# A 128-byte write by each DMA engine ahead of the first store of a streaming batch norm

## The chip, the cores and the metric

The kernel runs on one core of one Trainium2 chip. The metric is the device time of one execution in microseconds (us). It is limited by transfers: 537 MB go in and 537 MB go out.

## The reference

```
x: (32, 256, 128, 128) float32;  gamma, beta, running_mean, running_var: (256,)
out = gamma * (x - mean) / sqrt(var + 1e-5) + beta        # per channel
```

In the kernel this is one multiply and one add per element, with a scale and a shift per channel.

## The kernel before

The tensor is cut into 64 tiles of 128 channels x 16384 values (8 MB, 64 KB per partition). Three buffers go round. SyncE issues the loads, VectorE computes in place, ScalarE issues the stores. Each stream keeps one transfer in flight at a time; only the first two tiles' loads are queued without a wait.

```
nc.sync.dma_start(out=bufs[0][:, left], in_=xr[0][:, left]).then_inc(early, 16)   # a quarter of tile 0
zeroed = step(nc.vector.memset(rows[:], 0.0))
...                                        # four parameter loads of 16 rows x 1 KB
nc.sync.dma_start(out=bufs[0][:, right], in_=xr[0][:, right]).then_inc(loaded[0], 16)
for i in range(1, NT):
    s, turn = i % NBUF, i // NBUF
    if turn:
        nc.sync.wait_ge(stored[s], 16 * turn)              # the buffer is free
    inst = nc.sync.dma_start(out=bufs[s][:], in_=xr[i]).then_inc(loaded[s], 16)
    if i >= 2:
        inst._wait_ge(loaded[(i - 1) % NBUF], ...)         # the load before has landed
...                                        # scale and shift are made on VectorE and ScalarE
compute(0, left)._wait_ge(early, 16)
compute(0, right)._wait_ge(loaded[0], 16)
store(0, 2)                                                # a DMA issued by ScalarE
for i in range(1, last):
    compute(i)._wait_ge(loaded[i % NBUF], ...)
    turn_of_store(i)                                       # the store before has landed
    store(i, i + 2)
...                                        # the last tile is shared by VectorE and ScalarE
```

## Time and profile before

| | before |
|---|---|
| time, median of the first 3 runs | 2483.66 us (2483.18 to 2484.57) |
| span of the profiled execution | 2484.7 us |
| VectorE busy | 564.0 us (23%) |
| DMA queue of the loads / of the stores | 50.1% / 49.9% of the 16 engines' span |

The lines of the page that show this stand in the prediction. Two more things are used later. The first is what SyncE's DMA issues waited for, in the view of the DMA queue's own waits (us in total, times, longest). Line 98 waits for the load before, line 97 for the store that frees the buffer:

```profile
SPq L98 <- DMA t<-in_x_dram: 1378.8, 62, 48.0
SPq L97 <- DMA out_dram<-t: 1009.0, 61, 16.8
```

Each load waits for both, one after the other: first some 16.5 us for the store (1009.0 / 61), then some 22 us more for the load before (1378.8 / 62). So it is the load before that releases a load; its buffer has then been free for 22 us.

The second is the record of each DMA packet in the trace (start, duration, size, queue). A 64 KB packet is one row of a tile, and takes 2418 ns undisturbed. The records name no engine, but on a saturated engine each packet starts where the one before ended, so joining ends to starts gives sixteen rows. This is one of them around the first store (L load packet, S store packet; start in us + duration in ns):

```
before   L29.77+2419  L32.20+3072  S35.27+2418  L37.68+2418  S40.09+2418 ...
```

The load packet right before the first store packet is 654 ns too long. All 16 engines have such a packet, too long by 0.60 us on average. I call this "the stall before store 0" from here on; its size is always the excess over the undisturbed duration, summed over 16 engines' packets and divided by 16. Durations taken as undisturbed are 2418, 1815 and 608 ns for packets of 64, 48 and 16 KB.

### The profile page before, as it was taken

To read this page: it belongs to the slowest core of one execution; us is meant where nothing else is said; L and a number is where in the kernel's file an instruction comes from. 1 tells how busy PE (TensorE), PEld (TensorE's weight loads), DVE (VectorE), ACT (ScalarE), POOL (GpSimd) and SP (SyncE) were. 2 spreads that over 40 slices of the span, in tenths; PEclk is the share of its full clock that TensorE was granted. 3 is DMA by queue.
4 is the path that set the end of the run, shared out by engine and by line. 5 is a ranking of instruction groups with operands and counts; after the bars stand their busy time and mean duration, and the time that the engine had idled before them with its cause. 6 is when DMAs were issued, how large, how long until landed. Compare 5 with 4: busy or idle time off the path is not lost.

```text
span 2484.7 us, 389 instructions
## 1 busy us (share of the span) xinstructions
DVE 564.0 (23%) x76; ACT 7.9 (0%) x3; POOL 0.2 (0%) x4
## 2 busy tenths in 40 slices
DVE  3121221212212222122221221212212122121221
ACT  0000000000000000000000000000000000000001
POOL 0000000000000000000000000000000000000000
DMA  9999999999999999999999999999999999999999
GB/s 422 423 439 434 430 436 435 437 428 437 435 436 432 433 438 429 436 434 431 434 427 437 437 426 439 436 432 430 436 438 430 433 427 438 430 430 437 436 426 406
DMA packets 18707, 1073.84 MB, mean 432 GB/s; under 512 B 2128, under 2 KB 2192, under 8 KB 2192
## 3 DMA queue, kind: packets, MB, share of 16 engines
q1 hardware_dynamic: 9488, 536.94, 50.1%
q10 hardware_dynamic: 9216, 536.88, 49.9%
q14 instruction: 3, 0.02, 0.0%
HBM read 536.94 MB, written 536.87 MB: 432 GB/s over the span
## 4 chain that ended last, share of the span: by engine, by line
DMA 99%; ACT 0%; SPq 0%; issue 0%; DVE 0%; DVEq 0%
DMA t<-in_x_dram 99%; ACT t L154 0%; SPq L87 0%; DVE rows L85 0%; SPq L91 0%; DVE eps_t L103 0%; DVEq L190 0%; SPq L66 0%
## 5 line engine op out<-in xcount | busy, mean ns | idle before, releaser
L126 DVE TENSOR_SCALAR t<-t,scale_t,shift_t 128x16384 f32<-128x16384 f32 (+2 forms) x65 | 560.5, 8624 | 1886.5 <-DMA t<-in_x_dram 1886.4
L154 ACT ACTIVATE t<-t,shift_t,scale_t 128x7168 f32<-128x7168 f32 x1 | 6.4, 6361 | 2442.7 <-DMA t<-in_x_dram 2442.7
L104 DVE STREAM_TRANSPOSE turned<-rows 32x1024 f32<-32x1024 f32 x1 | 1.2, 1233 | 7.1 <-DMA rows<-in_running_mean_dram 7.1
L111 ACT ACT_TABLE_LOAD x1 | 1.3, 1283 | 0.9 <-SPq L66 0.9
L85 DVE MEMSET rows<- 32x1024 f32 x1 | 0.9, 912 | 1.2 <-SPq L66 1.2
L109 DVE COPY par<-turned 32x8 f32<-32x8 f32 x4 | 0.6, 162 | 0.1
L111 ACT ACTIVATE std_t<-par,eps_t 128x2 f32<-128x2 f32 x1 | 0.3, 295 | 9.2 <-DVE par L109 9.2
L118 DVE RECIPROCAL rstd_t<-std_t 128x2 f32<-128x2 f32 x1 | 0.2, 166 | 0.4 <-ACT std_t L111 0.4
L121 DVE TENSOR_TENSOR shift_t<-par,ms_t 128x2 f32<-128x2 f32 x1 | 0.2, 163 | 0.0
L120 DVE TENSOR_TENSOR ms_t<-par,scale_t 128x2 f32<-128x2 f32 x1 | 0.2, 161 | 0.0
L119 DVE TENSOR_TENSOR scale_t<-par,rstd_t 128x2 f32<-128x2 f32 x1 | 0.2, 161 | 0.0
L179 POOL MEMSET const-bfloat16-1.0<- 128x1 bf16 x1 | 0.1, 102 | 0.0
L179 POOL MEMSET const-uint8-127<- 128x1 uint8 x1 | 0.1, 101 | 0.0
L179 POOL MEMSET const-float32-0.0<- 128x1 f32 x1 | 0.1, 99 | 0.2 <-issue 0.2
L179 POOL MEMSET const-float32-1.0<- 128x1 f32 x1 | 0.1, 98 | 0.0
L103 DVE MEMSET eps_t<- 128x1 f32 x1 | 0.1, 59 | 0.1
## 6 DMA issues: line engine op xcount, KB each, us to landing
t<-in_x_dram SPq DMA_DIRECT2D x1, 6144.0 KB, 19.4
t<-in_x_dram SPq DMA_DIRECT2D x1, 2048.0 KB, 7.6
out_dram<-t ACTq DMA_DIRECT2D x64, 38.6
t<-in_x_dram SPq DMA_DIRECT2D x63, 38.6
rows<-in_running_var_dram SPq DMA_DIRECT2D x1, 16.0 KB, 6.4
rows<-in_gamma_dram SPq DMA_DIRECT2D x1, 16.0 KB, 6.2
rows<-in_beta_dram SPq DMA_DIRECT2D x1, 16.0 KB, 5.9
rows<-in_running_mean_dram SPq DMA_DIRECT2D x1, 16.0 KB, 5.9
```

What stands on the lines that cost most here:

```text
L85: zeroed = step(nc.vector.memset(rows[:], 0.0))
L103: step(nc.vector.memset(eps_t[:], eps))
L104: step(nc.vector.transpose(out=turned[:], in_=rows[:]), fetched, 16 * NPAR)
L109: placed = step(nc.vector.tensor_copy(out=flat[q * B : (q + 1) * B], in_=blocks[:, :, q, 0]))
L111: nc.scalar.activation(out=std_t[:], in_=var_t, func=mybir.ActivationFunctionType.Sqrt, bias=eps_t[:], scale=1.0,)._wait_ge(vec, placed).t ...
L118: step(nc.vector.reciprocal(out=rstd_t[:], in_=std_t[:]), act, 1)
L119: step(nc.vector.tensor_mul(out=scale_t[:], in0=gamma_t, in1=rstd_t[:]))
L120: step(nc.vector.tensor_mul(out=ms_t[:], in0=mean_t, in1=scale_t[:]))
L121: ready = step(nc.vector.tensor_sub(out=shift_t[:], in0=beta_t, in1=ms_t[:]))
L126: return nc.vector.tensor_scalar(out=t[:, cols], in0=t[:, cols], scalar1=scale_t[:, cb : cb + 1], scalar2=shift_t[:, cb : cb + 1], op0=myb ...
L154: nc.scalar.activation(out=t[:, VCOLS:], in_=t[:, VCOLS:], func=mybir.ActivationFunctionType.Identity, bias=shift_t[:, cb : cb + 1], scale ...
L179: nc = _bacc.Bacc("TRN2", target_bir_lowering=False, num_devices=1)
```

## The change

It means to take this first-store stall out of the stream of loads: each engine writes 128 bytes of zeros early, and store 0 covers them later. (Such a small early write is called a touch below.) Store 0 waits until they have landed, so that the order of the two writes is safe.

```
+    blank = params.tile([NE, B], f32, name="blank", tag="blank")          # 16 x 32
+    touched = tc.alloc_semaphore("touched")
...
+        blanked = step(nc.vector.memset(blank[:], 0.0))
+        nc.scalar.dma_start(out=outr[0][0 :: P // NE, 0:B], in_=blank[:])._wait_ge(vec, blanked).then_inc(touched, 16)
...
         compute(0, right)._wait_ge(loaded[0], 16)
+        nc.scalar.wait_ge(touched, 16)
         store(0, 2)
```

## The prediction

> **What bounds the kernel now.** I read the page first (busy shares, slices, queues, chain), then the windows view, the timeline of the first microseconds, the chain of waits in order of time, and last the DMA packet records of the trace one by one.
>
> ```profile
> span 2484.7 us, 389 instructions
> ## 1 busy us (share of the span) xinstructions
> DVE 564.0 (23%) x76; ACT 7.9 (0%) x3; POOL 0.2 (0%) x4
> ...
> DMA  9999999999999999999999999999999999999999
> ...
> q1 hardware_dynamic: 9488, 536.94, 50.1%
> q10 hardware_dynamic: 9216, 536.88, 49.9%
> ...
> DMA 99%; ACT 0%; SPq 0%; issue 0%; DVE 0%; DVEq 0%
> ```
>
> VectorE works 23% of the time. The 16 DMA engines are busy in every one of the 40 slices, and the two queues (q1 carries the loads that SyncE issues, q10 the stores that ScalarE issues) add up to 100% of the engines' time. So a microsecond is saved only if each DMA engine spends a microsecond less on its packets, or starts earlier, or ends closer to the end of the span.
>
> ```profile
> 0.00:2.00 2.00, 0.79 (x1) 1.10 (x1) 0.20 (x4) 1.00 0.07 16
> 2.00:4.00 2.00, 0.18 (x2) 0.18 (x1) 0.00 (x0) 1.00 0.98 344
> ...
> 80.00:2450.00 2370.00, 537.56 (x61) 0.00 (x0) 0.00 (x0) 1.00 1.00 433
> ...
> 2482.00:2484.70 2.70, 0.00 (x0) 0.00 (x0) 0.00 (x0) 1.00 0.00 0
> ```
>
> The last two columns are the DMA share and GB/s. The engines are idle for about the first 2.0 us and about the last 1.6 us, and saturated from 2 us on, before the first store exists. From the packet records: 16,256 packets of 64 KB take 2.418 us when nothing disturbs them. All of the data in such packets is 1073.74 MB / (16 x 64 KiB) = 1024 packets per engine, x 2.418 = 2476.0 us. Startup 2.0 and the tail 1.6 make 2479.6. The remaining 5.1 us of the span of 2484.7 are packets that took longer than 2.418 us, plus the small packets: summed over the records and divided by 16, the excess of load packets is 5.2 us (64 KB), 0.28 (48 KB) and 0.49 (16 KB), that of store packets 0.11. That is 6.1, 1 us more than the 5.1, since the records overlap slightly (on average 16.03 are open for 16 engines). This slack of some 5 to 6 us, 0.24% of the time, is all that any change to how packets flow can touch.
>
> **What the change aims at.** Listed by start, the excess has a peak just where the first store begins. Store 0 is issued at 30.04 us:
>
> ```profile
> 23.33 6.68 DVE L126 TENSOR_SCALAR t<-t,scale_t,shift_t 128x12288 f32<-128x12288 f32 x1 [8.31 <-DMA t<-in_x_dram]
> 30.04 78.75 ACTq L137 DMA_DIRECT2D out_dram<-t  x3
> 52.87 8.81 DVE L126 TENSOR_SCALAR t<-t,scale_t,shift_t 128x16384 f32<-128x16384 f32 x1 [22.86 <-DMA t<-in_x_dram]
> ```
>
> Its first 16 packets (one per engine) start 5.0 us after the issue; those of the next two stores start 4.0 us after theirs. The 16 load packets that stand right before them, one per engine, are long by 227 to 844 ns, 9.77 us in sum, so 0.61 us per engine. At the second, third and fourth store nothing of the kind stands in the records (excess per 20 us slice under 0.03 us). So something about the first write costs every engine about 0.61 us once. The change moves that first write ahead, to a 128-byte one.
>
> **What the Trainium skill says.** The page "DMA: Bandwidth & Descriptors", section "Queues, rings and completion order": each engine serves its queue rows in turn and switches only at packet boundaries. The trace agrees: packets of q1 and q10 fill the engines without overlap. The section "Why a DMA increments its semaphore by 16 and not by 1" says that the outermost size decides how many engines share a transfer: 16 rows make 16. The parameter loads of 16 rows agree: 64 packets of 1 KB for four of them, 16 each. Its section "Specifications" says that the engine does a read-modify-write for transfers under 512 B; this trace has no data write of that size. No page tells of a cost of an engine's first write; that stall is known here from the records alone.
>
> **The change part by part.**
> 1. One more memset on VectorE (16 x 32). The eps memset beside it takes 0.06 us; as every step waits for the one before, the setup chain becomes longer by about 0.1 us. That chain ends at 12.6 us, but the parameter transposition before it waits until 9.36 us for the fourth parameter load, so it is hidden there.
> 2. One more DMA issue on ScalarE. It takes about 0.35 us (the store issues take 0.34 to 0.37) and waits for the memset, so it starts at about 2.3 us. The built program shows it ahead of the activation table load, which goes from 0.90 to about 2.7 us and ends at 4.0; its result is wanted at 11.41. Hidden.
> 3. A wait for the landing of the 128-byte rows ahead of store 0. They land by about 6 to 10 us (parameter loads of 16 KB took 5.9 to 6.4 us to land); the store is ready at 30.04. Costs nothing.
> 4. Sixteen more data packets and 16 semaphore packets, one of each per engine. A 1 KB packet takes 46 ns and a semaphore packet 9 ns, so at most 0.06 us per engine.
> 5. The first-write stall at 35.5 us goes: -0.61 us.
> 6. The first-write stall comes back at the new place. The first load's issue starts at 0.95 and its first packet at 2.0 us, so the blank packet comes at about 2.3 + 1.0 = 3.3 to 3.5 us, when the engines have had load packets for 1.4 us (DMA share 0.98 in the window 2 to 4 us). There each engine does its own cold start: the first 16 load packets are long by 0.42 us on average, and end at 2.8 to 3.5 us. If the write stall falls into that, part is hidden; if it comes after, 0.61 is paid again, only earlier. Behind the small parameter packets the first 48 KB packets are long by 0.12 to 0.36 us, so a small transfer in the stream can cost such a bubble too: up to +0.28 us.
> Sum: -0.61 + 0.06 + (0 to 0.61) + (0 to 0.28), so -0.55 to +0.34 us. The middle is -0.1; I lean to some overlap and take -0.2.
>
> **The rivals.** (a) The stall is only moved: the engines are the bound at both places and never idle between, so the time stays at 2483.7 +- 0.3. For it: the share of 0.98 in the window in which the blank write arrives. (b) The stall is hidden in the startup of the reads or shrinks with a small packet: -0.55 us, 2483.1. For it: the cold reads of that very moment, and that a 128-byte packet holds little behind it. (c) The cost belongs to a store beside a 64 KB load packet, or to the first page of the output rather than the engine's first write, and appears at the first true store nevertheless: +0.06 to +0.3, 2483.9. Against it: stores 1 to 3 show none. (d) A new wait delays store 0 by a slow read-modify-write: it would need over 20 us to be felt, against 6 us for loads of 16 KB. Very unlikely. In none does the time move by even 0.05%.
>
> **Range and chances.** I predict 2483.66 - 0.2 = 2483.4 us. The spread of the runs is larger than the effect: the three runs cover 1.4 us, the profiled execution took 2486.4, and most of the 5.2 us of long load packets stand in irregular places (for example 1140 to 1300 us and 2040 to 2210 us), which may differ by run. So the range is 2482.2 to 2485.4. A change of 2% would be 49.7 us, nine times all of the slack there is, and a loss of that size would need the engines idle for 50 us, for which nothing is added. Faster 0.01, same 0.98, slower 0.01.
>
> **What would show it.** In the changed kernel's packet records: 16 packets of 128 B on q10 at about 3.5 us; the load packets around 35 us back to 2.418 us and store 0 first seen 4.0 to 4.4 us after its issue, not 5.0 (step 5 right); load packets around 3 to 6 us long by more than before (step 6, rival a) or not (rival b). If the packets before store 0 are still long, rival c holds. DMA share, queues and the chain stay at 99 to 100%. A change of over 2 us in the median of fast runs would prove the reading wrong.

## More of the kernel before

In the steady state a store is issued 16.9 us after a load and the next load 21.7 us after that (medians of the issue times). The two streams are staggered by about half of the 38.7 us that a tile takes.

## The result

| | before | changed |
|---|---|---|
| median of 6 runs | 2484.03 us | 2483.23 us |
| lowest to highest | 2482.88 to 2485.29 | 2482.53 to 2489.46 |
| span of the profiled execution | 2484.7 us | 2480.7 us |

The ratio of the fast runs is 1.0001, with a 95% interval of 0.9988 to 1.0014: the same. A ratio is the mean time of one kernel's fast runs over that of the other's of the same rounds, so it is not quite the ratio of the medians above; here one run of 2489.46 lifts the mean of the changed kernel.

The page of the changed kernel, in the parts that the prediction showed of the one before:

```profile
span 2480.7 us, 392 instructions
## 1 busy us (share of the span) xinstructions
DVE 564.1 (23%) x77; ACT 7.9 (0%) x3; POOL 0.2 (0%) x4
...
DMA  9999999999999999999999999999999999999999
...
q1 hardware_dynamic: 9488, 536.94, 50.0%
q10 hardware_dynamic: 9248, 536.88, 49.9%
...
DMA 99%; ACT 0%; issue 0%; SPq 0%; DVE 0%; DVEq 0%
```

One more VectorE instruction and 32 more packets on the store queue; nothing else has moved. The windows view (start and end, length, then engines, and at the end DMA share and GB/s):

```profile
0.00:2.00 2.00, 0.79 (x1) 0.00 (x0) 0.20 (x4) 1.00 0.18 41
2.00:4.00 2.00, 0.27 (x3) 1.28 (x1) 0.00 (x0) 1.00 0.97 328
...
80.00:2450.00 2370.00, 537.57 (x61) 0.00 (x0) 0.00 (x0) 1.00 1.00 434
...
2478.00:2480.70 2.70, 0.00 (x0) 0.00 (x0) 0.00 (x0) 1.00 0.00 0
```

The idle ends are as they were, and the middle runs at 434 GB/s against 433. The timeline of the changed kernel, at the start and around store 0 (start, length, engine, instruction):

```profile
2.18 0.09 DVE L105 MEMSET blank<- 16x32 f32 x1
2.30 0.38 ACTq L106 DMA_DIRECT2D out_dram<-blank  x1
...
2.71 1.28 ACT L117 ACT_TABLE_LOAD   x1 [2.71 <-DVE eps_t L109]
...
23.41 6.68 DVE L132 TENSOR_SCALAR t<-t,scale_t,shift_t 128x12288 f32<-128x12288 f32 x1 [8.25 <-DMA t<-in_x_dram]
30.12 0.36 ACTq L143 DMA_DIRECT2D out_dram<-t  x1
```

The write is issued at 2.30 us and the activation table is loaded after it, without harm. The page's part on DMA issues has the landing, 5.8 us after the issue, 22 us before anything asks for it:

```profile
out_dram<-blank ACTq DMA_DIRECT2D x1, 2.0 KB, 5.8
```

Now the packets around store 0, on one engine of each kernel:

```
before   L29.77+2419  L32.20+3072  S35.27+2418  L37.68+2418
changed  L29.80+2421  L32.22+3118  S35.33+2418  L37.74+2418
```

The stall is still there, at the same place. Over all 16 engines it was 0.60 us before and 0.75 us in the changed kernel. The early write itself left no mark: its 16 packets started between 5.74 and 6.99 us and took 13 ns each, and the 16 KB load packets of 5 to 8 us were long by 0.02 us in sum (0.04 before). The first 48 KB packets, at 7.6 to 8.1 us, were long by 0.28 us per engine (0.25 before).

Why then is the span 4.0 us shorter? The excess of all 64 KB load packets was 5.21 us per engine in the trace of before and 1.26 in the one of the changed kernel, 3.95 less. Before, most of it stood in places such as 1140 to 1300 us (1.2 us) and 2000 to 2240 us (1.4 us). The second trace of the kernel before (e8_before_again) and two variants of the changed kernel, below, tell whether the change has to do with this.

### The profile page after: what moved, and what is told of

It is laid out like the page before. It is cut to its first block, busy times and chain, and to the rows that moved or that the text cites. A ratio compares the mean times of both kernels' runs of the same rounds, so it can differ in the third digit from the quotient of the medians.

```text
span 2480.7 us, 392 instructions
## 1 busy us (share of the span) xinstructions
DVE 564.1 (23%) x77; ACT 7.9 (0%) x3; POOL 0.2 (0%) x4
## 4 chain that ended last, share of the span: by engine, by line
DMA 99%; ACT 0%; issue 0%; SPq 0%; DVE 0%; DVEq 0%
DMA t<-in_x_dram 99%; ACT t L161 0%; SPq L89 0%; DVE rows L87 0%; SPq L93 0%; DVE blank L105 0%; DVE eps_t L109 0%; DVEq L197 0%; SPq L68 0%
```

## The experiments

The question is why the early write did not take the stall away, and what the stall is. Two theories stood at first: the touch reached the wrong rows or came at the wrong time (then all rows, or a later touch, would help), or it was too small (then only a large early write would help). A third was that the stall isn't tied to the store at all. e1 to e3 and e9 to e12 are edits of the changed kernel; e4 to e7 are edits of the kernel before, without the 128-byte write, and e8 is the kernel before itself. In e4, e6 and e7 the load of tile 2 also waits for the early transfer, since that one uses its buffer.

### e1_shift: store 0 comes 10 us later

```
         nc.scalar.wait_ge(touched, 16)
+        for k in range(8):        # eight activations of 128x1024 on a tile that nobody uses
+            ...
         store(0, 2)
```

> The changed kernel with eight idle activations (128x1024, about 1 us each) on ScalarE ahead of store 0, so that store 0 is issued some 8 to 9 us later, at about 39 us, still within load 1. In the changed kernel the 16 load packets right before store 0 were long by 0.74 us per engine although the 128-byte rows had been written. If this stall belongs to the arrival of the first large store, the 16 long packets move with it to about 43 to 45 us and again cost 0.4 to 0.9 us per engine. If it belongs to a place in the run or in load 1, long packets stay at 33 to 36 us and those before store 0 are 2.418 us.

Store 0 was issued at 39.81 us. No load packet at 33 to 36 us was long, so the stall belongs to the store, not to a place in the run. But the store came just as the load of tile 1 ended. Its own first packets were long instead, by 0.69 us per engine. This can't be told from what later stores met in this run: each but the last has long packets, of 0.5 to 1.0 us per engine in sum. The run took 2587.87 us, 4.2% more than the kernel before on the same chip (2484.41). A delay of 10 us in one store cost 103 us. The timeline shows the new order (SPq issues loads, ACTq stores; x2 stands for two issues, from the start of the first to the end of the second):

```profile
39.81 41.46 ACTq L145 DMA_DIRECT2D out_dram<-t  x2
42.94 40.64 SPq L101 DMA_DIRECT2D t<-in_x_dram  x2
```

A store and the next load are now issued 3 us apart (2.4 us in the median later), no longer half a tile apart, and it stays so. The waits of SyncE's DMA issues (line 100 for the store, line 101 for the load before):

```profile
SPq L100 <- DMA out_dram<-t: 2288.8, 61, 38.5
SPq L101 <- DMA t<-in_x_dram: 188.4, 62, 38.1
```

A load now waits some 37.5 us for the store and then only 2.5 us for the load before (without the first wait of 38.1). It is still the load before that releases it, and each store is released by the store before; as a tile takes 40.4 us in both streams, the offset between them stays as it is. Both streams end and start anew within 2.4 us of each other, tile after tile, and most of the long packets stand at these starts: the excess in this trace is 48.3 us per engine on loads and 51.8 on stores, together 100.0 against 6.1 before, which is 93.9 of the 103 us. The windows view has 416 GB/s from 100 to 2500 us, in place of 433.

### e2_all_rows: 128 bytes to every row

```
-    blank = params.tile([NE, B], ...)          +    blank = params.tile([P, B], ...)
-    out=outr[0][0 :: P // NE, 0:B]             +    out=outr[0][:, 0:B]
```

> The changed kernel with the early write going to all 128 rows (128 bytes each, 8 packets per engine) with the same split over engines as the store, in place of every eighth row. If the 16-row touch failed because its rows fall to other engines than those that the store gives them to, the packets before store 0 go back to 2.418 us (stall under 0.1 us per engine). If a small write does not open what the first large store pays, the stall stays at 0.5 to 0.9 us per engine.

The stall before store 0 was 0.65 us, on all 16 engines. Which rows were touched was not what was wrong.

### e3_late_touch: the 128 bytes at 23 us

```
+        nc.scalar.wait_ge(loaded[0], 16)
         nc.scalar.dma_start(out=outr[0][0 :: P // NE, 0:B], in_=blank[:])...   # moved here, ahead of store 0
```

> The changed kernel with the 128-byte write issued only when load 0 has landed (about 23.4 us) in place of 2.3 us, so that it comes to the engines within 64 KB load packets and only some 8 us before store 0. If the early touch worked but was forgotten in the 29 us until store 0, the stall before store 0 goes (under 0.1 us), and may show up before the touch at about 27 us. If it is the first write that arrives behind 64 KB load packets that stalls them, whatever its size, the stall moves to about 27 us (0.5 us or more). If only a large write pays, it stays before store 0 at 0.5 to 0.9 us and nothing is long at 27 us.

The 16 small packets started at 27.4 to 27.8 us, 8 us before store 0, among load packets of 64 KB. None of those was long, and the stall before store 0 was 0.65 us. The touch was not forgotten; it had paid for nothing.

### e4_full_row: one 64 KB row per engine

```
+        nc.gpsimd.memset(bufs[2][0:NE, :], 0.0).then_inc(zeros, 1)      # the third buffer, not yet loaded
+        nc.scalar.dma_start(out=outr[0][0 :: P // NE, :], in_=bufs[2][0:NE, :])._wait_ge(zeros, 1).then_inc(touched, 16)
```

> The changed kernel with the early write being one whole 64 KB row per engine (16 rows of zeros from the still unused third buffer, zeroed by GpSimd), issued at about 18 to 22 us, during load 0. If the stall is a one-time cost of an engine's first large write, 16 load packets become long before it (0.4 to 0.9 us per engine at about 20 to 26 us) and those before store 0 are 2.418 us. If each first use of particular rows or of the first tile's buffer pays, the stall before store 0 stays at 0.5 to 0.9 us. The extra 1 MB adds 2.4 us to the time in either case.

Load packets before the early write were long by 0.55 us at 16 to 18 us, so a large write does meet the stall early. But store 0, which came at 41.7 us, met one of 0.49 us again. This fits neither expectation, and the run isn't clean: the 16 rows all came from partitions 0 to 15 and took up to 7.2 us in place of 2.4, an excess of 3.3 us per engine, and the load packets of 26 to 29 us, as they ended, were long by another 0.38. At this point "a long stretch of loads alone brings the stall back" was a theory of its own.

### e5_split_store: a part of store 0 comes early

```
-        store(0, 2)
+        nc.scalar.dma_start(out=outr[0][:, left], in_=bufs[0][:, left])._wait_ge(done, 1).then_inc(touched, 16)
+        nc.scalar.dma_start(out=outr[0][:, right], in_=bufs[0][:, right])._wait_ge(done, 2).then_inc(stored[0], 16)
```

> The kernel before with store 0 cut in two: its first quarter (128 rows of 16 KB) is issued when computed, at about 15 us, the rest at about 30 us. Theory G (the stall comes when a queue gets a large transfer after the engines have served only the other queue for a long time): load packets are long before the first part, at about 17 to 20 us (0.3 to 0.8 us per engine), and the second part, which comes some 5 us after the end of the first, finds no stall (under 0.15 us). Theory W (every first write to other bytes of the output by an engine pays): both parts pay 0.4 us or more. The time stays within 0.1% of before in either case.

(It has no blank write, and the fourth load also waits for the first part.) The first part met the stall in two portions, 0.17 us at 17 us and 0.45 us at 22 us, together 0.62; the second part met none. So it is one sum of about 0.6 us, paid once, and with packets of 16 KB it isn't paid all at the first of them. This speaks against a payment at every first write to other rows.

### e6_load_on_act and e7_quarter_touch: a load and a store at the same moment

```
e6  +   nc.scalar.dma_start(out=bufs[2][:, left], in_=xr[2][:, left]).then_inc(touched, 16)
e7  +   nc.scalar.dma_start(out=outr[0][:, left], in_=bufs[2][:, left])._wait_ge(zeros, 1).then_inc(touched, 16)
```

> The changed kernel with the early write replaced by an early load on ScalarE's queue: a quarter of tile 2 (128 rows of 16 KB), issued at about 12 us. If the stall comes from a second queue that starts while the other one is being served, whatever the direction, the load packets around 13 to 17 us are long by 0.3 us or more per engine. If it comes from writing to HBM, nothing is long there (under 0.1 us) and the stall before store 0 at about 32 to 38 us is as before (0.5 to 0.8 us). The extra 2 MB cost 4.8 us in the time.

> As e6_load_on_act, with a store of the same size at the same moment on the same queue (zeros from the unused third buffer to the first quarter of each row of tile 0). If writing is what stalls, the load packets at about 13 to 17 us are long by 0.3 to 0.8 us per engine here and not in e6_load_on_act. Then store 0 comes some 10 to 15 us after the end of this store: if one large write were enough for the whole run, the packets before it are 2.418 us; if a long stretch of loads alone brings the stall back, they are long by 0.3 to 0.8 us per engine. The extra 2 MB cost 4.8 us.

Both were issued on ScalarE's queue, with 2 MB, right after the same activation:

```profile
11.33 0.38 ACTq L150 DMA_DIRECT2D t<-in_x_dram  x1
```

```profile
11.55 0.37 ACTq L152 DMA_DIRECT2D out_dram<-t  x1
```

(The first line is of e6_load_on_act, the second of e7_quarter_touch, both from the timeline.) With the load, the load packets of 11 to 24 us were long by 0.03 us in sum, and the stall before store 0 was 0.68. With the store they were long by 0.66 us, and store 0 met none (0.00). A second queue that begins to work did not stall the first here; a write did. And this write paid for the later ones.

### e8_before_again: the kernel before once more

> The kernel before once more, unchanged, for a second trace. The stall before store 0 should be 0.5 to 0.8 us per engine again. The sum of all long load packets was 6.0 us per engine in the first trace of it and 2.2 in the one of the changed kernel; if that is a matter of the run and not of the change, it will differ here from 6.0 by a microsecond or more, or equal it by chance, and the time will move with it.

The stall before store 0 was 0.64 us. The excess of all load packets was 6.22 us against 5.98 in its first trace, at partly other places: 0.6 us at 740 to 760 us, where the first trace had none, and 0.2 in all at 1140 to 1300 us, where the first had 1.2. Of the changed kernel's variants, e2_all_rows had 6.36 and e3_late_touch 6.71. The low 2.22 of the changed kernel's own trace is therefore not what a 128-byte touch does; the 4.0 us between the two spans are the difference of two executions. The untraced times say so too: the fastest run of the kernel before (2482.88 us) is 0.35 us above the traced run of the changed one (2482.53), and in the rounds of e9 to e12 the kernel before once took 2489.65.

### e10_rows_4k and e11_rows_1k: how much must be written

```
-    blank = params.tile([NE, B], ...)     +  blank = params.tile([P, 1024], ...)    # e11: [P, 256]
-    out=outr[0][0 :: P // NE, 0:B]        +  out=outr[0][:, 0:1024]                 # e11: 0:256
```

> The changed kernel with an early write of 4 KB to each of the 128 rows, split over the engines as the store is (8 packets, 32 KB per engine), issued at about 3 us. So far: 128-byte touches paid nothing and saved nothing, a quarter of a tile (16 KB to each of 128 rows) paid 0.65 us once and freed store 0, which came 7 us after its end; a full row per engine (16 rows) paid 0.55 and store 0, 17 us later, paid 0.49 again. Theory D (dose: the stall is paid over the first 20 to 40 KB that an engine writes, once): about 0.5 us per engine of long load packets at 6 to 22 us, and under 0.15 before store 0. Theory F (a stretch of some 15 us of loads alone brings it back): the same at 6 to 22 us, and again 0.5 to 0.8 before store 0. Theory L (only packets of 16 KB and more pay): nothing extra early and 0.5 to 0.8 before store 0.

> As e10_rows_4k with 1 KB to each row (8 KB per engine), issued at about 2.5 us. Theory D: a part of the stall early (0.1 to 0.3 us per engine) and the rest before store 0 (0.3 to 0.5). Theories F and L: 0.5 to 0.8 before store 0 whatever was paid early.

One engine of e10_rows_4k, early and around store 0 (its 4 KB store packets, of 159 ns, are left out):

```
e10   L4.46+611  L5.10+935  L6.04+1032  L7.36+813 ...  L31.61+2419  L34.02+2429  S36.45+2418  L38.86+2418
```

With 32 KB per engine in packets of 4 KB, the 16 KB load packets of 5 to 9 us were long by 0.94 us per engine (0.02 to 0.05 in the kernels with early touches of 128 bytes), and store 0, some 30 us later, met none. So the stall is moved by this touch. Not all of the 0.94 comes on top: the first 48 KB load packets, long by 0.2 to 0.4 us per engine without such a write, are long by 0.02 here. Over all load packets of the first 14 us the excess is 1.60 us, and 1.41 in e12_far_rows, against 0.75 to 1.06 in the kernels with no early write or one of 128 bytes. The difference, some 0.4 to 0.8 us, is about what store 0 is spared (0.60 to 0.75). The touch also takes 8 x 159 ns = 1.27 us of each engine. The load of the rest of tile 0, on which the compute waits, lands 2.1 us later, and so store 0 is issued at 32.25 us in place of 30.12:

```profile
25.54 6.68 DVE L132 TENSOR_SCALAR t<-t,scale_t,shift_t 128x12288 f32<-128x12288 f32 x1 [8.96 <-DMA t<-in_x_dram]
32.25 0.34 ACTq L143 DMA_DIRECT2D out_dram<-t  x1
```

With 8 KB per engine in packets of 1 KB (e11_rows_1k), 0.14 us was paid at 5 to 9 us on 16 KB packets, nothing over all load packets of the first 14 us (0.79), and store 0 met 1.18 us, more than without any touch. Theory D expected a remainder of 0.3 to 0.5 us, so it is wrong in this: the payment isn't shared out in proportion to bytes. Whether the amount per engine counts (over 8, at most 32 KB) or the size of a packet (over 1, at most 4 KB), these two runs do not tell, because both sizes grew together. Neither can be the whole of it: one packet of 64 KB per engine (e4_full_row) is above both and did not free store 0.

### e9_rows_4k_later: a longer stretch of loads alone

```
-            if i >= 2:                    +            if i > 2:          # the load of tile 2 no longer waits for tile 1
+        eight short activations ahead of store 0, as in e1_shift
```

> As e10_rows_4k, with store 0 held back by eight short activations (8 to 9 us) and the load of tile 2 issued without waiting for tile 1, so that loads follow one another without a gap and the stretch of loads alone between the early write and store 0 is 9 us longer than in e10_rows_4k. Theory D: no stall before store 0 (under 0.15 us) if e10_rows_4k has none. Theory F: 0.5 to 0.8 us before store 0, which then stands at about 43 to 46 us. Theory L as in e10_rows_4k. The time itself may be longer by up to 4%, as in e1_shift, where the same delay put loads and stores in step.

1.07 us was paid at 5 to 9 us on 16 KB packets, and the load packets right before store 0, at 46.2 us, were not long (0.01). Some 38 us of loads nearly alone did not bring the stall back, so that theory falls. What store 0 met in e4_full_row remains unexplained. My bound for the time was wrong: the run took 3030.45 us, 22% more, not 4%. The second load of the two queued at the start lands early. From then on a load is released by the landing of a store, which also releases the next store, and the streams fell into step still more tightly (x3: from the start of the first to the end of the third):

```profile
93.67 102.28 ACTq L143 DMA_DIRECT2D out_dram<-t  x3
93.68 102.22 SPq L100 DMA_DIRECT2D t<-in_x_dram  x3
```

Store and load were issued 0.01 us apart, and a tile took some 51.5 us. From about 1800 us on the load before landed just after the store, the next load was issued 0.1 us after the next store, and a tile took 42.7 us. Why so small an offset should matter stays open. The page shows both halves:

```profile
DMA  9898989888898989898889889999999999999999
GB/s 389 312 350 315 342 309 338 313 330 328 317 340 319 340 312 345 304 339 318 336 309 339 312 346 388 388 409 389 391 385 393 403 386 388 393 407 390 385 386 407
```

The span is 544 us longer than in the trace of the kernel before. The packets' records add up to 2763.7 us per engine, 280 more than there, nearly all of it excess (285 against 6.1). For the rest, some 261 us, the engines stood without a packet, where the kernel before had them busy throughout.

### e12_far_rows: the same write, 336 MB away

```
-    out=outr[0][:, 0:1024]                +    out=outr[40][:, 0:1024]              # as e10, but the rows of tile 40
```

> As e10_rows_4k (4 KB to each of 128 rows, 32 KB per engine, issued at about 3 us), but into the rows of tile 40 of the output, 336 MB away from tile 0, which the later store of tile 40 covers. In e10_rows_4k the stall was paid at 4 to 8 us (0.9 us per engine) and store 0 found none. If what is paid belongs to the engines and their first writes of some size, wherever they go, store 0 finds no stall here either (under 0.15 us). If it belongs to the part of the output that is written (its first rows), store 0 finds 0.5 to 0.8 us or more, and store 40 none.

0.84 us was paid at 5 to 9 us, and store 0 met none (0.00). So the stall isn't tied to the output's first rows, or to any address that was tried. Whether the engines pay it, or the way from SBUF or to HBM, is not shown.

| run | early write per engine | paid early, us per engine | stall before store 0 | time, us |
|---|---|---|---|---|
| before, and e8_before_again | none | 0.04, 0.02 | 0.60, 0.64 | 2486.43, 2486.14 |
| changed | 128 B | 0.02 | 0.75 | 2482.53 |
| e2_all_rows | 8 x 128 B | 0.05 | 0.65 | 2486.35 |
| e3_late_touch | 128 B at 27 us | none seen | 0.65 | 2486.36 |
| e6_load_on_act | a load, 8 x 16 KB | 0.03 | 0.68 | 2492.44 |
| e11_rows_1k | 8 x 1 KB | 0.14 | 1.18 | 2486.26 |
| e10_rows_4k | 8 x 4 KB | 0.94 | 0.00 | 2485.30 |
| e12_far_rows | 8 x 4 KB, far away | 0.84 | 0.00 | 2485.20 |
| e9_rows_4k_later | 8 x 4 KB | 1.07 | 0.01 | 3030.45 |
| e7_quarter_touch | 8 x 16 KB | 0.66 | 0.00 | 2489.43 |
| e5_split_store | 8 x 16 KB, part of store 0 | 0.62 | 0.00 (second part) | 2487.08 |
| e4_full_row | 1 x 64 KB, 16 partitions | 0.55 | 0.49 | 2491.99 |

("Paid early" is the excess of the 16 KB load packets at about 4.5 to 9 us, to within 0.01; in e6 and e7 that of all load packets of 11 to 24 us, in e4 of those at 16 to 18 us. The time is that of the traced execution.) e6, e7 and e4 took 8.0, 5.0 and 7.6 us more than the kernel before in their rounds (2484.41), where 4.8, 4.8 and 2.4 had been expected for their extra bytes. No kernel here is faster than the kernel before beyond doubt: e10 and e12 are single executions within the range of the kernel before (2482.88 to 2489.65). Nothing in the table takes the payment out of the saturated stretch, and whether it would vanish in idle time, as in the first 2 us, no run tried.

## Why the prediction was right or wrong

**The time and the bound: right.** The 16 engines stayed saturated, the queues stayed at 50% each, and 2483.23 us lies 0.2 us from the 2483.4 of the prediction. That closeness proves little: the six runs of one kernel spread over 2.4 us and of the other over 6.9, and the effect looked for is 0.6. What was right is the argument that made the range narrow, that all slow packets together are some 6 us and that a saturated engine has no idle time in which to hide a payment.

**Steps 1 to 4: right in substance.** The memset took 0.09 us (0.06 foreseen) and the first compute started 0.13 us later (12.74 after 12.61; 0.1 foreseen). The issue at 2.30 us and the table load from 2.71 to 3.99 came as worked out, and hurt nothing. The landing at 8.1 us left 22 us of room. The added packets cost 13 + 9 ns per engine, below the 0.06 us allowed.

**Step 5: wrong.** "The first-write stall at 35.5 us goes: -0.61 us" is the step that failed. It took the first write, of any size, for what costs. The runs show that writes of 128 bytes and 1 KB per row leave the stall at 0.65 to 1.18 us, and that 8 writes of 4 KB or 16 KB per engine take it away (0.00 to 0.01). The prediction said itself that no page and no line tells of the cost; it then took the change's intent for the mechanism.

**Step 6: wrong in place, and void in cost.** The blank packets came at 5.74 to 6.99 us, not at 3.3 to 3.5: the 1.0 us from issue to first packet was taken from the first load, whose engines were idle. With 16 KB load packets ahead of it the write took 3.4 us, and in the steady state 3.9 us is usual. No stall moved there, as this write pays none, and no bubble was added either: all 48 KB load packets were long by 0.32 us per engine in sum, 0.28 before. The sum of 5 and 6 came out near zero because both were zero, not because they cancelled. That the time was foreseen so closely is luck in this respect.

**The rivals.** Rival (c), that the cost "appears at the first true store nevertheless", is what happened, in its words on the profile: packets before store 0 still long. It is right in that a small touch doesn't open what the store pays, and its other half, the first page of the output, is refuted for store 0 by e12_far_rows. The prediction held against it that "stores 1 to 3 show none", which does not speak against it: a payment that a first large write makes once also leaves stores 1 to 3 free. Rival (a), "only moved", is what a larger touch does (e10_rows_4k); the change never got that far.

**Readings and sums.** Some small ones of the prediction are off, and nothing rests on them. The 16 long packets exceed 2418 ns by 9.57 us in sum (0.60 each), not 9.77. The fourth store's slice has an excess of 0.06 us, not under 0.03. The first 16 load packets end by 3.65 us, not 3.5. 2483.66 - 0.2 is 2483.46. In the account of the slack the small packets (1.4 us per engine) are missing from the 6.1, so the records add up to 2.5 us more than the time, not 1.

**What stays open.** Why an engine's first tens of KB of writes cost the loads before them some 0.6 us, why the 1 KB touch made it 1.18, why a 64 KB row per engine did not free store 0 in e4_full_row, and whether the 0.6 us is time lost or only a delay between reading and writing that any store stream must have. No record of a trace shows inside an engine.

## What to carry to other kernels

When a change is meant to pay a one-time cost early, first check that the early operation pays it: one look at the packets before the first real use tells. Moving such a cost within the saturated stretch showed no gain here. And before you delay or speed up the start of one of two streams with one transfer in flight each, look at the offset between them: here half a period apart took 38.7 us a tile, 2.4 us apart 40.4. A single late store cost this kernel 4%, over a hundred times what the change was after.

## What the Trainium skill lacked or had wrong

- Page "DMA: Bandwidth & Descriptors": nothing on a cost of an engine's first larger writes. Here load packets lost 0.60 to 0.75 us per engine before the first store, and not before the second and third, as long as the two streams were half a period apart; 8 packets of 4 KB per engine were enough to pay for it; 8 of 1 KB were not, nor was one of 64 KB.
- The same page, section "Issuing engines are not separate DMA queues", says that transfers of different issuers share the 16 engines and interleave. It says nothing on the phase of two streams: with a load and a store issued 17 and 22 us apart in turn a tile took 38.7 us, with them 2.4 us apart 40.4 us, and with both issued together 51.5 us (0.01 us apart) or 42.7 us (0.1 us apart).
- The same page, section "Latency and other measured facts", gives about 600 ns to the first byte for DMAs issued from SyncE and ScalarE. On idle engines the first packet came 0.65 us after the end of the issue (1.03 after its start), which agrees. What the page lacks is the wait on busy engines: from the start of the issue it was 3.4 us beside load packets of 16 KB, and about 3.9 us between packets of 64 KB.
- The same page, section "Specifications", says that transfers under 512 B are read-modify-write. The 128-byte packets took 13 ns each in the records and the 16 KB load packets beside them were long by no more than before (0.02 against 0.04 us), so no run here shows a cost of it.
